# S5 angles on GpSimd, and accumulation groups of u opened by one-pass products with zeros

## The chip, the core and the metric

The kernel runs on one core of one Trainium2 chip, in one launch. The core's engines have queues of their own and wait for each other through semaphores: TensorE (PE in the profile, its weight loads PEld), VectorE (DVE), ScalarE (ACT), GpSimd (POOL) and SyncE (SP), whose queue issues all loads from the chip's memory. The metric is the device time of one execution in microseconds; less is better.

## The reference, cut to what matters

The whole program is a network of three layers over 256 tokens of width 2048 in float32: a state-space layer (S5), a sparse attention layer, and a block with two mixers and a feed-forward part. The change lies in the first, at its beginning:

```
c_act = silu(c)
shift, scale, gate = split(c_act @ mod_w[0] + mod_b[0], 3)
h = rmsnorm(x, norm_g[0]) * (1 + scale) + shift
u, z = split(h @ w_in, 2)
a = exp(lam * dt)            # complex, 128 groups of 64 states; its angle is Im(lam) * dt
x_t = a * x_(t-1) + B u_t    # a scan over the tokens
```

The kernel runs the scan over blocks of four tokens. For it, it needs the angle k * 4 * Im(lam) * dt in turns, brought into -0.5 to 0.5, for k = 0 to 63 and every state: 16 tiles of 128 partitions x 256 columns. These are the S5 angles.

## The kernel before, in words

**The stage of u.** `layer0` makes u, 2048 features x 256 tokens, from h, which is there in 16 pieces h(k) of 128 features. u is held in eight PSUM tiles `ua0` to `ua7` of 128 x 512 while k runs from 0 to 15, and each k adds 16 products (L469, float32, each shown as two records in the trace). So that the two halves of each tile form one accumulation group, a product of a row of zeros with zeros opens it (L448 to L450): `zero` is a tile of one partition and 512 columns, filled by GpSimd, and there is one product of 128 x 512 for each of the eight tiles.

**h(k).** For every k, two vectors of 128 numbers are made from 1 MB of weights each: `mod_ahead` loads a tile `w` of 128 x 2048 (four buffers) and VectorE multiplies it with a row and sums along it (L345, the row product). The first gives the scale (L458 makes A from it), L460 makes `hTf` from x, the second gives the shift, L349 adds the bias, and ScalarE writes h(k) (L463). The weights of u for that k are two loads `wu` of 0.5 MB, three buffers for each half.

**The angles.** Inside the same loop over k stand `s5_angles` for tile k and, for every fourth k, `s5_scaled_b`. In `s5_angles` ScalarE writes two parts of the product, `pa` (kept in `yraw`, four L677 with `fh`) and `pb` (a tile `angb`, four L677 with `fl`), and then five operations of VectorE (L678 to L682) make the sum, its rounded value `pr` (a tile `angr`), the difference, and the limits. `angb` and `angr` have two buffers each. `s5_scaled_b` is six GpSimd operations (L695 to L700), and its two work tiles `bw` are taken from the same buffers as `angb` and `angr`.

**What sets the order.** The program is written as above, and a scheduler orders the instructions of each engine when the kernel is built; after that each engine runs its queue in order. All 64 L677 with `fh` come early; those with `fl` stand between the L463 of the h(k).

**Behind the stage.** u is copied out of PSUM by ScalarE (L488) and VectorE (L486), sent to the chip's memory and read back in another layout; the PSUM tiles are then given to other work, so that the first product of z (L192) comes after the last copy. Three z products stand before the S5 loop over 16 tiles. It reads the angles of tile ut in L783 and L784, which make cosine and sine tables, and for each tile GpSimd, VectorE and ScalarE make small matrices (L743 to L760), the first two tiles' in the stage of u.

Of the kernel before, what the change touches and what calls it, by code (L numbers as in the profile page):

```python
# [10 lines left out]
F32R = mybir.dt.float32r  # L11
I32 = mybir.dt.int32
AF = mybir.ActivationFunctionType
ALU = mybir.AluOpType
# [4 lines left out]
P = 128  # L19
# [4 lines left out]
MAGIC = 12582912.0  # L24
# [15 lines left out]
def build(tc, a, dbg=None, upto=99):  # L40
    with ExitStack() as ctx:
        g = Ctx()
        g.ctx, g.tc, g.nc, g.a, g.dbg = ctx, tc, tc.nc, a, dbg or {}
        setup(g)
        with tc.tile_pool(name="cactp", bufs=1) as g.cactp:
            layer0(g)
            if upto >= 1:
                layer1(g)
        if upto >= 2:
            block2(g, upto)  # L50
        else:
            save_out(g)
            close_x(g)
            if upto:
                g.ucm.__exit__(None, None, None)
            else:
                close_xT(g)
            g.pscm.__exit__(None, None, None)
# [114 lines left out]
def proj_one(g, src, hl):  # L173

    nc = g.nc
    o = g.mm.tile([P, 2, T], F32, name="o", tag="mm")[:, 0, :]
    wk = split_w(g, src, 2048, P)
    for k in range(KD):
        h, l = wk(k)
        nc.tensor.matmul(o, h, hl[:, k, 0, :], start=(k == 0), stop=False)  # L180
        nc.tensor.matmul(o, h, hl[:, k, 1, :], start=False, stop=False)  # L181
        nc.tensor.matmul(o, l, hl[:, k, 0, :], start=False, stop=(k == KD - 1))  # L182
    return o
# [209 lines left out]
def layer0(g):  # L393
    nc, tc, a = g.nc, g.tc, g.a
    V, S, G, E = nc.vector, nc.scalar, nc.gpsimd, nc.tensor
    with ExitStack() as lc:
# [50 lines left out]
        zero = g.sp.tile([P, 512], F32, name="zero", tag="res", bufs=2)[0:1]  # L447
        G.memset(zero, 0.0)  # L448
        for o in acc:
            E.matmul(o, zero[:, 0:P], zero, start=True, stop=False)  # L450
        sc = ExitStack()
        s1 = sc.enter_context(tc.tile_pool(name="l0s1", bufs=1, reuse_waits="tile"))
        with tc.tile_pool(name="l0tmp", bufs=1, reuse_waits="tile") as tmp:
# [1 line left out]
        with tc.tile_pool(name="l0raw", bufs=2, reuse_waits="tile") as rp:  # L455
            for k in range(KD):
                mod_ahead(g, a["mod0"], g.mod0, 16 + k)
                V.scalar_tensor_tensor(out=A0[:, k:k + 1], in0=g.mod0[:, 16 + k:17 + k], scalar=b1[:, k:k + 1], in1=col("norm_g0")[:, k:k + 1], op0=ALU.add, op1=ALU.mult)  # L458
                f = g.sp.tile([P, T], F32, name="hTf", tag="t1k")
                V.scalar_tensor_tensor(out=f, in0=xT[:, k, :], scalar=A0[:, k:k + 1], in1=row, op0=ALU.mult, op1=ALU.mult)  # L460
                mod_ahead(g, a["mod0"], g.mod0, k)
                mod_bias(g, g.mod0, col("mod_b0"), k, k + 1)
                S.activation(out=h[:, k, :], in_=f, func=AF.Identity, bias=g.mod0[:, k:k + 1])  # L463
                for hf, pool in enumerate((g.whp, g.wlp)):
                    w = pool.tile([P, 1024], F32R, name="wu", tag=("wh", "wl")[hf]).bitcast(F32)
                    load = nc.sync.dma_start(out=w, in_=a["w_inu"][k, :, hf * 1024:(hf + 1) * 1024])
                    for i in range(8):
                        m = 8 * hf + i
                        E.matmul(acc[m // 2][:, m % 2, :], w[:, i * P:(i + 1) * P], h[:, k, :], start=False, stop=(k == KD - 1 and m % 2 == 1))  # L469
                s5_angles(g, s5, rp, k, yraw)  # L470
                if k % 4 == 1:
                    s5_scaled_b(g, s5, rp, k // 4, ybuf)
            g.after = load.ins
# [65 lines left out]
        for j in range(KD):  # L539
            o = proj_one(g, a["w_glu"][j], y)  # L540
# [127 lines left out]
def s5_angles(g, R, pool, ut, ang):  # L668

    nc = g.nc  # L670
    tl = lambda nm, sh: pool.tile(sh, F32, name=nm, tag=nm)
    ts4 = slice(4 * ut, 4 * ut + 4)
    pa = ang[:, ut, :].rearrange("p (a k) -> p a k", a=4)
    pb, pr = tl("angb", [P, 4, 64]), tl("angr", [P, 4, 64])
    for i in range(4):
        for f, out in ((R.fh, pa), (R.fl, pb)):
            nc.scalar.activation(out=out[:, i, :], in_=R.km[:, 0, :], func=AF.Copy, scale=f[:, 4 * ut + i:4 * ut + i + 1])  # L677
    nc.vector.tensor_tensor(out=pr, in0=pa, in1=pb, op=ALU.add)  # L678
    nc.vector.tensor_scalar(out=pr, in0=pr, scalar1=MAGIC, scalar2=-MAGIC, op0=ALU.add, op1=ALU.add)
    nc.vector.tensor_tensor(out=pa, in0=pa, in1=pr, op=ALU.subtract)  # L680
    nc.vector.tensor_tensor(out=pa, in0=pa, in1=pb, op=ALU.add)
    nc.vector.tensor_scalar(out=pa, in0=pa, scalar1=0.5, scalar2=-0.5, op0=ALU.min, op1=ALU.max)  # L682


def s5_scaled_b(g, R, pool, q, bb):
# [1128 lines left out]
```

## Time and profile before

| | us |
|---|---|
| median of 3 runs | 2939.35 |
| lowest, highest | 2933.03, 2940.2 |
| the profiled execution | 2936.83 |
| its span, first to last instruction | 2935.0 |
| TensorE busy (matmuls) | 2809.1 |
| VectorE busy | 2064.6 |
| ScalarE busy | 1434.3 |
| GpSimd busy | 478.6 |

The table says which engine has most work over the whole span; which one a stage waits for is another question, and is read from that stage alone. The rows below are therefore almost all of the first 170 us. Times in them are microseconds from the span's start, durations of single operations are in ns where the row says so. A span of GpSimd is rougher than those of the other engines.

### The profile page before, as it was taken

To read this page: it belongs to the slowest core of one execution; us is meant where nothing else is said; L and a number is where in the kernel's file an instruction comes from. 1 tells how busy PE (TensorE), PEld (TensorE's weight loads), DVE (VectorE), ACT (ScalarE), POOL (GpSimd) and SP (SyncE) were. 2 spreads that over 40 slices of the span, in tenths; PEclk is the share of its full clock that TensorE was granted. 3 is DMA by queue.
4 is the path that set the end of the run, shared out by engine and by line. 5 is a ranking of instruction groups with operands and counts; after the bars stand their busy time and mean duration, and the time that the engine had idled before them with its cause. 6 is when DMAs were issued, how large, how long until landed. Compare 5 with 4: busy or idle time off the path is not lost.

```text
span 2935.0 us, 41793 instructions
## 1 busy us (share of the span) xinstructions
PE 2809.1 (96%) x15680; PEld 2425.4 (83%) x15680; DVE 2064.6 (70%) x3400; ACT 1434.3 (49%) x2879; POOL 478.6 (16%) x465
## 2 busy tenths in 40 slices
PE   7989988998999999999999998999999999999998
PEld 5878878876778888888888897788888888888887
DVE  8958897878787777766997685666656665456654
ACT  5337765433345555555555454455444444344443
POOL 1325652210000011012020020111101211002110
PEclk8999988998999999999999999999999999999999
DMA  9964555986975555555544343355655555555553
GB/s 369 394 225 163 182 192 200 351 305 251 338 277 211 199 195 189 204 208 200 184 152 149 125 143 120 127 189 188 231 184 187 187 190 196 187 188 193 193 187 143
DMA packets 111995, 608.75 MB, mean 207 GB/s; under 512 B 27848, under 2 KB 34480, under 8 KB 41648
## 3 DMA queue, kind: packets, MB, share of 16 engines
q1 hardware_dynamic: 111792, 606.08, 57.6%
q8 instruction: 123, 2.02, 0.3%
q14 instruction: 80, 0.66, 0.1%
HBM read 597.23 MB, written 8.79 MB: 206 GB/s over the span
## 4 chain that ended last, share of the span: by engine, by line
PE 76%; DVE 9%; ACT 3%; DMA 3%; issue 2%; POOL 1%; SPq 0%; ACTq 0%; DVEq 0%; POOLq 0%
PE o L168 29%; PE o L169 15%; PE ox L228 6%; PE ox L230 6%; PE ox L229 6%; PE o L1211 2%; DVE wl L143 2%; DVE w L345 2%; PE o L1212 1%; ACT wh L140 1%; PE o L192 1%; DMA w<-in_mod_dram 1%; DMA w<-in_w_kvT_dram 1%; PE o L182 1%; PE o L181 1%
## 5 line engine op out<-in xcount | busy, mean ns | idle before, releaser
L143 DVE TENSOR_TENSOR wl<-w,wh 128x1024 fp32r<-128x1024 f32 x778 | 971.1, 1252 | 645.0 <-ACT wh L140 639.8
L140 ACT CAST wh<-w 128x1024 fp32r<-128x1024 f32 x778 | 812.8, 1048 | 983.1 <-PE o L168 486.0
L168 PE MATMUL o<-u,wh 128*128 128x512 f32 x2704 | 951.0, 395 | 1.0 <-DVE qk L204 0.4
L169 PE MATMUL o<-u,wl 128*128 128x256 f32 x2704 | 761.1, 282 | 2.7 <-DVE ci L1331 2.7
L168 PEld LDWEIGHTS o<-u,wh 128*128 128x128 f32 x2704 | 508.1, 188 | 115.3 <-PE ctr L1343 1.5
L169 PEld LDWEIGHTS o<-u,wl 128*128 128x128 f32 x2704 | 508.4, 188 | 5.1 <-DVE ci L1331 3.1
L168 PE MATMUL o<-hq,wh 128*128 128x512 f32 (+1 forms) x1040 | 374.5, 401 | 3.0 <-DVE hq L339 2.0
L345 DVE SCALAR_TENSOR_TENSOR w<-w,cact 128x2048 f32<-128x2048 f32 x128 | 301.5, 2357 | 41.5 <-DMA w<-in_mod_dram 20.2
L169 PE MATMUL o<-hq,wl 128*128 128x256 f32 (+1 forms) x1040 | 297.5, 286 | 0.0
L168 PEld LDWEIGHTS o<-hq,wh 128*128 128x128 f32 (+1 forms) x1040 | 195.0, 188 | 51.4 <-DVE hq L339 3.4
L169 PEld LDWEIGHTS o<-hq,wl 128*128 128x128 f32 (+1 forms) x1040 | 195.0, 187 | 2.2 <-DVE wl L143 0.2
L228 PE MATMUL ox<-wh,hid 128*128 128x512 f32 x352 | 138.5, 394 | 0.0
L229 PE MATMUL ox<-wh,hid 128*128 128x512 f32 x352 | 137.0, 389 | 0.0
L1190 POOL TENSOR_TENSOR half<-half,gt 128x256 f32<-128x256 f32 x44 | 32.8, 745 | 583.1 <-PE o L168 286.5
L230 PE MATMUL ox<-wl,hid 128*128 128x512 f32 x352 | 125.7, 391 | 0.0
L192 PE MATMUL o<-h,w 128*128 128x256 f32 x512 | 122.9, 395 | 2.1 <-DVE h L486 2.1
L469 PE MATMUL ua<-h,wu 128*128 128x256 f32 x512 | 115.5, 389 | 4.4 <-ACT h L463 4.4
L469 PEld LDWEIGHTS ua<-h,wu 128*128 128x128 f32 x512 | 100.0, 196 | 21.0 <-ACT h L463 5.2
L192 PEld LDWEIGHTS o<-h,w 128*128 128x128 f32 x512 | 99.1, 199 | 15.9 <-DVE h L486 2.5
L168 PE MATMUL o<-hkv,wh 128*128 128x512 f32 x256 | 96.2, 414 | 10.8 <-DVE hkv L339 5.7
L1060 POOL TENSOR_TENSOR om<-om 128x256 f32<-128x256 f32 x16 | 11.8, 734 | 493.9 <-DVE om L1058 341.5
L198 ACT COPY half<-o 128x256 f32<-128x256 f32 (+1 forms) x190 | 68.8, 364 | 30.8 <-PE o L169 27.7
(540 smaller groups left out, 4844.4 us busy)
## 6 DMA issues: line engine op xcount, KB each, us to landing
w<-in_mod_dram SPq DMA_DIRECT2D x96, 1024.0 KB, 6.9
w<-in_w_z_dram SPq DMA_DIRECT2D x48, 1024.0 KB, 4.9
w<-in_w_fg_dram SPq DMA_DIRECT2D x44, 1024.0 KB, 5.0
w<-in_w_fu_dram SPq DMA_DIRECT2D x44, 1024.0 KB, 4.9
w<-in_w_fd_dram SPq DMA_DIRECT2D x44, 1024.0 KB, 4.9
w<-in_kvmod_dram SPq DMA_DIRECT2D x32, 1024.0 KB, 6.3
w<-in_w_out_dram SPq DMA_DIRECT2D x32, 1024.0 KB, 5.6
w<-in_w_qkvz_dram SPq DMA_DIRECT2D x32, 1024.0 KB, 4.9
```

The lines of the kernel that those rows point to most:

```text
L140: nc.scalar.copy(out=wh[:, :step], in_=w)
L143: eng.tensor_tensor(out=wl[:, :step], in0=w, in1=wh[:, :step].bitcast(F32), op=ALU.subtract)
L168: nc.tensor.matmul(o[:m], h, hl[:, k0 + k, :, :], start=(k == 0), stop=False)
L169: nc.tensor.matmul(o[:m, 1, :], l, hl[:, k0 + k, 0, :], start=False, stop=(k == nk - 1))
L192: nc.tensor.matmul(o, w[:, k * P:(k + 1) * P], h[:, k, :], start=(k == 0), stop=(k == KD - 1))
L198: g.nc.scalar.copy(out=t[:m], in_=o[:m, 0, :])
L228: nc.tensor.matmul(ot, h, wh, start=first, stop=False)
L229: nc.tensor.matmul(ot, l, wh, start=False, stop=False)
L230: nc.tensor.matmul(ot, h, wl, start=False, stop=last)
L345: g.nc.vector.scalar_tensor_tensor(out=w, in0=w, scalar=1.0, in1=g.cact, op0=ALU.mult, op1=ALU.mult, accum_out=cols[:, j:j + 1])
L469: E.matmul(acc[m // 2][:, m % 2, :], w[:, i * P:(i + 1) * P], h[:, k, :], start=False, stop=(k == KD - 1 and m % 2 == 1))
L1211: nc.tensor.matmul(o, h[:, sl], hl[k][:, 0, :, :], start=(k == 0), stop=False)
```

## The change

The openers read the zeros as float32r, which TensorE takes in one pass, in place of float32; and the five operations of the angles go from VectorE's queue to GpSimd's:

```
         for o in acc:
-            E.matmul(o, zero[:, 0:P], zero, start=True, stop=False)
+            E.matmul(o, zero[:, 0:P].bitcast(F32R), zero.bitcast(F32R), start=True, stop=False)
...
-    nc.vector.tensor_tensor(out=pr, in0=pa, in1=pb, op=ALU.add)
-    nc.vector.tensor_scalar(out=pr, in0=pr, scalar1=MAGIC, scalar2=-MAGIC, op0=ALU.add, op1=ALU.add)
-    nc.vector.tensor_tensor(out=pa, in0=pa, in1=pr, op=ALU.subtract)
-    nc.vector.tensor_tensor(out=pa, in0=pa, in1=pb, op=ALU.add)
-    nc.vector.tensor_scalar(out=pa, in0=pa, scalar1=0.5, scalar2=-0.5, op0=ALU.min, op1=ALU.max)
+    nc.gpsimd.tensor_tensor(out=pr, in0=pa, in1=pb, op=ALU.add)
+    nc.gpsimd.tensor_scalar(out=pr, in0=pr, scalar1=MAGIC, scalar2=-MAGIC, op0=ALU.add, op1=ALU.add)
+    nc.gpsimd.tensor_tensor(out=pa, in0=pa, in1=pr, op=ALU.subtract)
+    nc.gpsimd.tensor_tensor(out=pa, in0=pa, in1=pb, op=ALU.add)
+    nc.gpsimd.tensor_scalar(out=pa, in0=pa, scalar1=0.5, scalar2=-0.5, op0=ALU.min, op1=ALU.max)
```

The scheduler then orders the other instructions anew too, up to the end of the S5 loop.

GpSimd's queue at the start of the stage, before. The names are those of the kernel with a number for each buffer; `bw_450` and `bw_451` are the work tiles of `s5_scaled_b`.

```order
L448 MEMSET zero_232 1x512
L695 ISA
L695 TENSOR_TENSOR bw_450<-braw_448,cre_339 128x256
L696 TENSOR_TENSOR bw_451<-braw_448,cim_340 128x256
L697 TENSOR_TENSOR ybuf_220<-bw_450,bw_451 128x4x64
L698 TENSOR_TENSOR bw_450<-braw_448,cre_339 128x256
L699 TENSOR_TENSOR bw_451<-braw_448,cim_340 128x256
L700 TENSOR_TENSOR ybuf_220<-bw_450,bw_451 128x4x64
```

The same place now, `angb_387` and `angb_433` being the angles' parts of tiles 0 and 1:

```order
L678 TENSOR_TENSOR angr_388<-yraw_219,angb_387 128x256
L679 TENSOR_SCALAR angr_388<-angr_388 128x256
L678 TENSOR_TENSOR angr_434<-yraw_219,angb_433 128x256
L680 TENSOR_TENSOR yraw_219<-yraw_219,angr_388 128x256
L679 TENSOR_SCALAR angr_434<-angr_434 128x256
L681 TENSOR_TENSOR yraw_219<-yraw_219,angb_387 128x256
L680 TENSOR_TENSOR yraw_219<-yraw_219,angr_434 128x256
L682 TENSOR_SCALAR yraw_219<-yraw_219 128x256
L681 TENSOR_TENSOR yraw_219<-yraw_219,angb_433 128x256
L682 TENSOR_SCALAR yraw_219<-yraw_219 128x256
L695 TENSOR_TENSOR bw_450<-braw_448,cre_339 128x256
L696 TENSOR_TENSOR bw_451<-braw_448,cim_340 128x256
```

The ten operations of the first two tiles stand before `s5_scaled_b`, and the others follow between its groups: 104 operations up to the last angle, where there were 24.

ScalarE's queue towards the end of the stage, before. `hTf_896`, `hTf_942`, `hTf_988` and `hTf_1044` lead to h(11) to h(14); `angb_1071` and `angb_1117` are tiles 14 and 15.

```order
L463 ACTIVATE h_118<-hTf_896,mod0_215 128x256
L677 ACTIVATE angb_1071<-km_350,fl_317 128x64 x4
L463 ACTIVATE h_118<-hTf_942,mod0_215 128x256
L677 ACTIVATE angb_1117<-km_350,fl_317 128x64 x4
L496 COPY d32_1195<-col_116 32x16 x4
L783 ACTIVATE ys_1237<-yraw_219 128x256
L790 ACTIVATE d0_1241<-km_350,r4_296 128x64 x4
L790 ACTIVATE d0_1388<-km_350,r4_296 128x64 x4
L785 ACTIVATE cs_1236<-ys_1237,hpi_325 128x256
L463 ACTIVATE h_118<-hTf_988,mod0_215 128x256
```

The same place now:

```order
L463 ACTIVATE h_118<-hTf_896,mod0_215 128x256
L677 ACTIVATE angb_1015<-km_350,fl_317 128x64 x4
L463 ACTIVATE h_118<-hTf_942,mod0_215 128x256
L677 ACTIVATE angb_1071<-km_350,fl_317 128x64 x4
L677 ACTIVATE angb_1117<-km_350,fl_317 128x64 x4
L463 ACTIVATE h_118<-hTf_988,mod0_215 128x256
L496 COPY d32_1195<-col_116 32x16 x4
L783 ACTIVATE ys_1237<-yraw_219 128x256
L790 ACTIVATE d0_1241<-km_350,r4_296 128x64 x4
L790 ACTIVATE d0_1388<-km_350,r4_296 128x64 x4
L785 ACTIVATE cs_1236<-ys_1237,hpi_325 128x256
L463 ACTIVATE h_118<-hTf_1044,mod0_215 128x256
```

h(13) moved ahead of L496 to L785, h(14) stands behind them; what the L677 before each of them wait for was VectorE (and for some a GpSimd operation of `s5_scaled_b`), and is now GpSimd alone. h(13) stands behind the L677 of tile 15, which needs GpSimd's 95th operation, the last of the fourth `s5_scaled_b`; L496 needs the 100th.

VectorE's queue in the middle of the stage, before: from the second row product of k=8 to the first of k=9.

```order
L345 SCALAR_TENSOR_TENSOR w_750,mod0_215<-w_750,cact_88 128x2048
L678 TENSOR_TENSOR angr_684<-yraw_219,angb_683 128x256
L349 TENSOR_TENSOR mod0_215<-mod0_215,col_116 128x1
L679 TENSOR_SCALAR angr_684<-angr_684 128x256
L680 TENSOR_TENSOR yraw_219<-yraw_219,angr_684 128x256
L681 TENSOR_TENSOR yraw_219<-yraw_219,angb_683 128x256
L682 TENSOR_SCALAR yraw_219<-yraw_219 128x256
L345 SCALAR_TENSOR_TENSOR w_790,mod0_215<-w_790,cact_88 128x2048
```

The same place now, and the next row product:

```order
L345 SCALAR_TENSOR_TENSOR w_750,mod0_215<-w_750,cact_88 128x2048
L349 TENSOR_TENSOR mod0_215<-mod0_215,col_116 128x1
L345 SCALAR_TENSOR_TENSOR w_790,mod0_215<-w_790,cact_88 128x2048
L458 SCALAR_TENSOR_TENSOR A0_216<-mod0_215,b1_217,col_116 128x1
L460 SCALAR_TENSOR_TENSOR hTf_794<-h_118,A0_216,rrow_210 128x256
L345 SCALAR_TENSOR_TENSOR w_796,mod0_215<-w_796,cact_88 128x2048
```

The operations of the angles are gone from between the row products; for each k there are left two L345, L458, L460 and L349.

## Rows read from the trace of the kernel before

**Rows 1.** The page's first line.

```profile
span 2935.0 us, 41793 instructions
```

**Rows 2.** Stretches: length; PE, PEld, DVE, ACT, POOL busy (instructions); PEclk, DMA share, GB/s.

```profile
28.00:42.00 14.00, 13.45 (x17) 5.14 (x16) 12.12 (x43) 10.55 (x36) 0.00 (x0) 0.50 0.88 353
42.00:50.00 8.00, 8.00 (x24) 6.15 (x24) 8.00 (x18) 8.00 (x34) 0.00 (x0) 0.64 0.94 338
50.00:100.00 50.00, 50.00 (x233) 44.03 (x232) 49.21 (x90) 16.89 (x62) 14.86 (x16) 1.00 1.02 404
100.00:150.00 50.00, 49.24 (x227) 42.68 (x226) 49.23 (x79) 16.54 (x58) 23.58 (x21) 1.00 0.99 385
150.00:160.00 10.00, 6.32 (x22) 5.33 (x23) 9.05 (x19) 3.48 (x10) 7.05 (x9) 0.83 0.51 174
```

**Rows 3.** TensorE in order of time: start, us, what, [idle before <-releaser].

```profile
28.64 13.99 PE L450 MATMUL ua<-zero 1*128 1x512 f32 x16 [0.55 <-ACT rrow L327]
...
42.56 92.61 PE L469 MATMUL ua<-h,wu 128*128 128x256 f32 x416
135.68 14.08 PE L469 MATMUL ua<-h,wu 128*128 128x256 f32 x64 [0.52 <-ACT h L463]
153.68 8.79 PE L469 MATMUL ua<-h,wu 128*128 128x256 f32 x32 [3.92 <-ACT h L463]
164.54 20.99 PE L192 MATMUL o<-h,w 128*128 128x256 f32 x96 [2.07 <-DVE h L486]
```

**Rows 4.** VectorE's angle operations and L345: ns min/median/max, first and last start.

```profile
L678 DVE TENSOR_TENSOR angr<-yraw,angb x16: 415/420/834, 55.0 to 129.8; 128x256 f32<-128x256 f32 x16
L679 DVE TENSOR_SCALAR angr<-angr x16: 280/286/707, 55.8 to 130.6; 128x256 f32<-128x256 f32 x16
...
L345 DVE SCALAR_TENSOR_TENSOR w<-w,cact x128: 2227/2285/3341, 15.1 to 1249.1; 128x2048 f32<-128x2048 f32 x128
```

**Rows 5.** Who waited for whom, 50 to 165 us: total, times, longest.

```profile
ACT h L463 <- DVE mod L349: 44.3, 10, 6.4
ACT angb L677 <- DVE yraw L681: 18.1, 9, 4.2
```

**Rows 6.** GpSimd in order of time, `s5_scaled_b`.

```profile
81.38 2.55 POOL L698 TENSOR_TENSOR bw<-braw,cre 128x256 f32<-128x256 f32 x1
...
97.36 0.79 POOL L695 TENSOR_TENSOR bw<-braw,cre 128x256 f32<-128x256 f32 x1 [12.00 <-DVE yraw L682]
...
101.24 2.85 POOL L700 TENSOR_TENSOR ybuf<-bw 128x256 f32<-128x256 f32 x1
```

**Rows 7.** VectorE in order of time, beside GpSimd, and at the stage's end.

```profile
80.64 2.81 DVE L345 SCALAR_TENSOR_TENSOR w<-w,cact 128x2048 f32<-128x2048 f32 x1
...
83.38 0.70 DVE L682 TENSOR_SCALAR yraw<-yraw 128x256 f32<-128x256 f32 x1
84.00 0.57 DVE L458 SCALAR_TENSOR_TENSOR A<-mod,b,col 128x1 f32<-128x1 f32 x1
84.61 1.03 DVE L460 SCALAR_TENSOR_TENSOR hTf<-h,A,rrow 128x256 f32<-128x256 f32 x1
...
161.52 2.28 DVE L345 SCALAR_TENSOR_TENSOR w<-w,cact 128x2048 f32<-128x2048 f32 x1
```

**Rows 8.** GpSimd alone: ns min/median/max of L1060; a memset, busy and mean ns.

```profile
L1060 POOL TENSOR_TENSOR om<-om x16: 724/735/737, 900.9 to 1300.5; 128x256 f32<-128x256 f32 x16
...
L859 POOL MEMSET Vc<- 128x512 f32 x1 | 0.5, 524 | 25.3 <-DVE res L995 25.3
```

**Rows 9.** L345 alone from 53 to 151 us (each shows twice: product and sum).

```profile
53.00:151.00 98.00, 51.55 (x44) 1.00 0.99 395
```

**Rows 10.** ScalarE in order of time.

```profile
51.29 2.00 ACT L677 ACTIVATE angb<-km,fl 128x64 f32<-128x64 f32 x8
...
128.41 0.89 ACT L496 COPY d<-col 32x16 f32<-32x16 f32 x4
...
131.56 0.49 ACT L785 ACTIVATE cs<-ys,hpi 128x256 f32<-128x256 f32 x1
```

## The prediction

> **What bounds the kernel now.** I read the table of stretches first, then TensorE's own order of time, then the waits and the orders of ScalarE, GpSimd and VectorE in the stage that the change touches. The profiled execution spans 2935.0 us [rows 1]; the change lies in its first 170 us, the stage that makes u. TensorE opens the eight accumulation groups from 28.64 to 42.63 us, then runs the u products without a gap: 416 records, 13 values of k, in 92.61 us, so 7.12 us for one k [rows 3]. It waits 0.52 us before k=13 and 3.92 us before k=15, takes 8.79 us for the last k, and is done with u at 162.47 [rows 3]. Both waits end with ScalarE's L463, which writes h(k). The table of stretches says why h comes late: VectorE is busy 49.2 of 50 us in both 50 us stretches [rows 2], and L463 waited 44.3 us in all for VectorE's L349, the bias behind the row product of L345 [rows 5]. The DMA queues are nearly full as well (404 and 385 GB/s [rows 2]). So this stage is bound by VectorE, with the loads and TensorE close behind. A microsecond more or less here moves the end by about as much, since the loop after it cannot start before u is copied out (the first L192 at 164.54 [rows 3]).
>
> **The openers.** Before: 16 records in 13.99 us at a granted clock of 0.50 [rows 2, 3]. No row shows a one-pass opener. The records halve to eight; if a record keeps its 0.87 us (13.99 / 16), the openers take 7.0 us, and TensorE reaches k=0 near 35.6. The bounds are no gain (0) and all of it (14 us). It is worth 7 us only where TensorE stays the last to arrive. From 35.6, k=9 is due at 35.6 + 9 x 7.12 = 99.7 us, or up to 6 us later if the clock stays at 0.50 until 47.8 as now (a mean of 0.64 from 42 to 50 us is 5.8 us at 0.50 [rows 2]). Below, h(9) is not there by then, so I count the openers at nothing. Their cover is the late h; were that gone, they would be worth the 7 us.
>
> **What VectorE gives away.** 16 tiles of five operations: three with two tensors at 0.42 us and two with one tensor at 0.286 us [rows 4], 16 x 1.83 = 29 us of work out of a full engine. If GpSimd ran beside VectorE this would be a clear gain. It doesn't run beside it here.
>
> **What GpSimd takes.** 80 operations are put in front of and between the 24 of s5_scaled_b. Three prices are needed.
> An operation with two tensors: five starts from 97.36 to 101.24 us, with only short VectorE work between, are (101.24 - 97.36) / 5 = 0.776 us apart [rows 6]; alone one lasts 0.735 us [rows 8].
> An operation with one tensor and two constants has no row on GpSimd. Below it lies a plain memset of 128x512 at 0.524 us, half of which is 0.26 us for 256 columns [rows 8]; above it the 0.776 us. VectorE's ratio, 0.286 / 0.42 = 0.68 [rows 4], puts it at 0.53 us, which is what I take, midway between the ends.
> The Trainium skill (GPSIMD Engine Reference, section 3.1, Elementwise — side-by-side cycle accounting) gives a body with one input about 1.03 cycles an element against 2.6 with two. At that page's 1.2 GHz my estimate from it is 0.735 - 256 x 1.57 / 1200 = 0.40 us; the sum below would then be 3.6 us smaller. No run here shows it.
> Third, what a row product costs GpSimd. When L345 (2.285 us [rows 4]) runs, a GpSimd operation that has begun doesn't end until it is over: spans of 2.55 and 2.85 us at 81.38 and 101.24 in place of 0.735 [rows 6], so 1.82 to 2.12 us lost for each L345, 1.95 taken. The reverse also holds: beside GpSimd's operations VectorE's L682, L458 and L460 take 0.70, 0.57 and 1.03 us, one after the other, and the L345 before them 2.81 us [rows 7]. That is about 0.45 us for each GpSimd operation, so 95 of them put 43 us back on VectorE, more than the 29 us taken off. VectorE is not relieved either.
>
> **Where the path goes.** ScalarE's order decides who waits. Its four L677 for tile k write angb, which has two buffers, also used by s5_scaled_b; they wait until GpSimd has read the buffer two uses before. h(k) stands behind them in the same queue. By the order, h(9) stands behind GpSimd's operation 46 of 104, h(13) behind operation 95, and h(14) behind operation 100 and 3.6 us of other ScalarE work (L496 to L785, 128.41 to 132.05 [rows 10]). GpSimd can begin when the first angb is written, about 52.3 us (ScalarE comes to it at 51.29 [rows 10], and nothing before that moves).
> Operation 46: 33 x 0.776 + 13 x 0.53 = 32.5 us, and some 12 row products at 1.95 = 23.4, so 52.3 + 55.9 = 108.2, later than TensorE wants k=9.
> Operation 95: 67 of the two-tensor kind and 28 of the other, 52.0 + 14.8 = 66.8 us. Row products in that time: 22 lie from 53 to 151 us now [rows 9] and are all that remain of the 32; at least 18 must be over, since h(13) itself needs the first 28. I take 20: 39.0 us. 52.3 + 66.8 + 39.0 = 158.1 us. One more group of four L677 (1.0 us) and L463 (0.5 us) give k=13 at about 159.7; it began at 135.68.
> h(14), after five more operations (3.5 us), one or two row products and the 3.6 us, comes at 167 to 169, when k=13 has just ended. Then 3 x 7.12 = 21.4 us, and the 1.7 us that the k after a gap took longer (8.79 against 7.12 [rows 3], the clock 0.83 on the mean in that stretch [rows 2]): u is done at 182.8 in place of 162.47, **20.3 us later**.
> The tail: an L345 that stood at 161.52 before the last two copies of u [rows 7] comes after them, worth at most 0.9 us, left out. GpSimd's work for the first two tiles (L743 to L760) now starts some 20 us later too, near 166, but TensorE needs it only after three z products, 21 us (96 records in 20.99 us [rows 3]) past the end of u: covered by more than 20 us; without that cover it would cost its own 10 us. Behind that, the S5 loop has the same work in a slightly different order; nothing prices that, 0 taken, 8 us either way for the range.
> Against the profiled execution (2936.83 us, of which 2935.0 is the span) the sum is 2957; that execution is 2.5 us under the median of the runs, 2939.35. From the median: 2939.35 + 20.3 = **2960 us**.
>
> **The rivals.**
> A, GpSimd keeps pace: it fits its operations between the row products, ScalarE never waits for it, and VectorE is 20 us ahead. TensorE is then the bound: 35.6 + 16 x 7.12 and 2.9 us for the slow clock at the start (5.8 us at half speed, as above) give 152.4, 10.1 us earlier: 2929 us. For it: VectorE's 99% is what h waits for now. Against it: every L345 that met a waiting GpSimd operation held it to its end. The Trainium skill (SBUF — State Buffer, section Who interferes with whom) says that a VectorE instruction with two inputs in SBUF contends with a GpSimd one that reads SBUF, and that the later one blocks fully; by that rule A is out, and the trace agrees with its 2.85 us.
> B, GpSimd is late, but less: if about half the row products cost it nothing, because it waits for ScalarE or a load at that time anyway, operation 95 comes 10 to 20 us earlier, the openers' 7 us count in part, and u ends within 9 us of now: 2931 to 2948. For it: GpSimd depends on ScalarE's angb, so its idle times may fall under L345.
> C, it is worse: the one-tensor operation costs 1.0 us on GpSimd (28 x 0.47 = 13 us) or the S5 loop loses 8 us by its new order: 2968 to 2981. For it: no row shows that operation on GpSimd.
> Which side it falls on is decided by operation 95: the change is a gain if it is over before about 134 us, a loss after about 142.
>
> **How the numbers follow.** Forecast 0.60, A 0.10, B 0.13, C 0.17. About 0.3%, 9 us, is what a measurement of this kernel can tell from no change. A alone is faster by more than that, B alone within it: faster 0.10, same 0.13, slower 0.77. The forecast's own ends: one-tensor operations at 0.26 or 0.776 us (-7.6, +6.9), 18 or 22 row products (3.9), 1.82 or 2.12 for each (-2.6, +3.4), the S5 loop (8): about 13 us together, 2947 to 2973. The range is widened to take half of B and nearly all of C: 2944 to 2981.
>
> **What would show it.** In the profile after: GpSimd busy nearly throughout from 52 us to beyond 155, with spans of 2.5 us and more on L678 to L682; VectorE's short operations still stretched; ScalarE's L677 waiting for GpSimd's L681 and L700 for tens of us in place of 18.1 us for VectorE [rows 5]; TensorE in gaps before L463 from k=9 on and k=13 near 160; openers of about 7 us. The forecast is wrong if L463 still waits mostly for L349, if angles end before 145, or if TensorE runs u without gaps.

## The result

The changed kernel takes 2960.78 us (median of 6 runs, 2951.64 to 2962.87), and the kernel before in the same comparison 2932.42 us (median of 6, 2925.58 to 2940.2): a ratio of 1.0083, 95% interval 1.0069 to 1.0098. The forecast was 2960 us, slower. It is slower by 28.4 us, where the sum had 20.3 from a median of 2939.35: that the two times lie within 1 us of each other is luck, since the base came out 6.9 us lower than the sum took it and the rise 8.1 us larger. Four of the six runs took 2959 to 2963 us, the traced one among them (2962.74), and two 2952.

The profile after. Its span, then TensorE's order of time (start, duration, line, how many, and in brackets the idle time before and what ended it), against [rows 1, 3]:

```profile
span 2960.9 us, 41771 instructions
```

```profile
29.41 3.75 PE L450 MATMUL ua<-zero 1*128 1x512 f32 x8 [0.55 <-ACT rrow L327]
33.09 44.67 PE L469 MATMUL ua<-h,wu 128*128 128x256 f32 x192
80.56 8.60 PE L469 MATMUL ua<-h,wu 128*128 128x256 f32 x32 [2.81 <-ACT h L463]
92.46 15.77 PE L469 MATMUL ua<-h,wu 128*128 128x256 f32 x64 [3.30 <-ACT h L463]
108.77 7.17 PE L469 MATMUL ua<-h,wu 128*128 128x256 f32 x32 [0.55 <-ACT h L463]
129.97 23.30 PE L469 MATMUL ua<-h,wu 128*128 128x256 f32 x96 [14.02 <-ACT h L463]
160.79 9.44 PE L469 MATMUL ua<-h,wu 128*128 128x256 f32 x32 [7.52 <-ACT h L463]
171.68 14.08 PE L469 MATMUL ua<-h,wu 128*128 128x256 f32 x64 [1.45 <-ACT h L463]
187.94 22.67 PE L192 MATMUL o<-h,w 128*128 128x256 f32 x96 [2.19 <-DVE h L486]
```

The reader sees the openers take 3.75 us in place of 13.99, TensorE begin u 9.5 us earlier, and lose that and more in gaps that all end with L463: 14.02 us before k=10, 7.52 before k=13. u ends at 185.76, and z begins 23.4 us later than before. The waits from 50 to 190 us (us in total, times, longest), against [rows 5], and the table of stretches (the pairs of numbers are TensorE, its weight loads, VectorE, ScalarE and GpSimd, then the granted clock, the DMA share and GB/s), against [rows 2]:

```profile
ACT angb L677 <- POOL yraw L681: 48.3, 7, 9.9
DVE w L345 <- DMA w<-in_mod_dram: 37.7, 14, 10.7
PE ua L469 <- ACT h L463: 29.6, 6, 14.0
ACT angb L677 <- POOL ybuf L700: 20.4, 4, 7.2
```

```profile
50.00:100.00 50.00, 43.90 (x188) 37.51 (x187) 37.74 (x48) 14.06 (x52) 45.58 (x36) 0.93 0.92 364
100.00:150.00 50.00, 35.43 (x153) 30.14 (x152) 23.14 (x27) 8.83 (x32) 48.93 (x52) 0.86 0.71 272
```

L463 no longer waits for L349. ScalarE waits 68.7 us for GpSimd (48.3 + 20.4) with h(k) queued behind it, GpSimd is busy 94.5 of 100 us, and VectorE, which had 98.4 [rows 2], only 60.9. VectorE is idle in large part because its loads are late: it waits 37.7 us for `w`. One reason stands in SyncE's queue (issues, none of them between the second row and the third), and what it does in VectorE's:

```profile
112.52 3.78 SPq L466 DMA_DIRECT2D wu<-in_w_inu_dram  x2
116.40 0.38 SPq L122 DMA_DIRECT2D w<-in_mod_dram  x1
133.66 0.33 SPq L691 DMA_DIRECT2D braw<-in_s5b_dram  x1
134.08 0.38 SPq L122 DMA_DIRECT2D w<-in_mod_dram  x1
...
SPq L691 <- POOL bw L699: 25.2, 3, 16.8
...
139.10 2.30 DVE L345 SCALAR_TENSOR_TENSOR w<-w,cact 128x2048 f32<-128x2048 f32 x1 [10.66 <-DMA w<-in_mod_dram]
```

`braw` has one buffer. Its next load (L691) waits 16.8 us for the late L699 on GpSimd, and the loads of `w` and `wu` behind it in the queue wait with it. It is not the only reason: the same queue waits 58.7 us for TensorE to free buffers of `wu` (L466, shown with the run with four buffers for `braw`). So GpSimd's lateness reaches h by two queues, ScalarE's and SyncE's.

GpSimd itself: the rounding and the clamp (duration in ns, min/median/max), and four of its spans:

```profile
L679 POOL TENSOR_SCALAR angr<-angr x16: 1062/1094/3217, 54.2 to 165.8; 128x256 f32<-128x256 f32 x16
L682 POOL TENSOR_SCALAR yraw<-yraw x16: 393/399/2503, 65.1 to 169.4; 128x256 f32<-128x256 f32 x16
```

```profile
54.24 3.06 POOL L679 TENSOR_SCALAR angr<-angr 128x256 f32<-128x256 f32 x1
57.27 2.67 POOL L678 TENSOR_TENSOR angr<-yraw,angb 128x256 f32<-128x256 f32 x1
59.91 0.72 POOL L680 TENSOR_TENSOR yraw<-yraw,angr 128x256 f32<-128x256 f32 x1
60.60 3.10 POOL L679 TENSOR_SCALAR angr<-angr 128x256 f32<-128x256 f32 x1
```

I added up all of GpSimd's spans on L678 to L700 up to the last angle, and counted as held those over 1.9 us, each with what it has above the shortest of its line: 117.1 us of spans, of which 22 held ones make 42.2 us, 1.92 each. The rest, 74.9 us, is GpSimd's own work.

### The profile page after: what moved, and what is told of

The parts are those of the page before. It is cut to its first block, busy times and chain, and to the rows that moved or that the text cites. A ratio compares the mean times of both kernels' runs of the same rounds, so it can differ in the third digit from the quotient of the medians.

```text
span 2960.9 us, 41771 instructions
## 1 busy us (share of the span) xinstructions
PE 2808.6 (95%) x15672; PEld 2429.6 (82%) x15672; DVE 2042.7 (69%) x3320; ACT 1433.6 (48%) x2879; POOL 564.9 (19%) x545
## 4 chain that ended last, share of the span: by engine, by line
PE 76%; DVE 10%; POOL 5%; ACT 4%; DMA 3%; issue 2%; SPq 0%; ACTq 0%; DVEq 0%; POOLq 0%
PE o L168 29%; PE o L169 15%; PE ox L230 6%; PE ox L228 6%; PE ox L229 6%; PE o L1211 2%; DVE wl L143 2%; DVE w L345 2%; DMA w<-in_mod_dram 1%; PE o L192 1%; PE o L1212 1%; POOL angr L679 1%; PE o L182 1%; PE o L181 1%; PE o L180 1%
## 5 line engine op out<-in xcount | busy, mean ns | idle before, releaser
L345 DVE SCALAR_TENSOR_TENSOR w<-w,cact 128x2048 f32<-128x2048 f32 x128 | 304.9, 2383 | 71.3 <-DMA w<-in_mod_dram 59.3
L469 PE MATMUL ua<-h,wu 128*128 128x256 f32 x512 | 123.0, 405 | 29.6 <-ACT h L463 29.6
L1060 POOL TENSOR_TENSOR om<-om 128x256 f32<-128x256 f32 x16 | 11.8, 735 | 490.4 <-DVE om L1058 341.5
L180 PE MATMUL o<-y,wh 128*128 128x256 f32 x256 | 74.6, 297 | 10.6 <-ACT z L501 4.9
```

The lines of the kernel that those rows point to most:

```text
L345: g.nc.vector.scalar_tensor_tensor(out=w, in0=w, scalar=1.0, in1=g.cact, op0=ALU.mult, op1=ALU.mult, accum_out=cols[:, j:j + 1])
```

## The experiments

The theory going in: the angles alone make the loss; a row product (L345) that meets a GpSimd operation holds it, GpSimd's chain falls behind, and the queues that wait for it bring h late. The rivals: the openers take part in it; GpSimd's own work is simply too much; VectorE, slowed beside GpSimd, is the path. Ratios are against the kernel before on the same chip, with 95% intervals.

**The openers alone.**

```
-            E.matmul(o, zero[:, 0:P], zero, start=True, stop=False)
+            E.matmul(o, zero[:, 0:P].bitcast(F32R), zero.bitcast(F32R), start=True, stop=False)
```

> The kernel before with the one-pass openers alone; the angles stay on VectorE. Theory (the openers were counted at nothing because h is late): TensorE reaches k=0 near 33 us in place of 42.6, runs into a late h from about k=9 on and then follows VectorE, so u ends 0 to 4 us earlier: 2928 to 2933 us against 2932.4. Rival 1 (TensorE is the bound of this stage): the whole 10 us, 2922. Rival 2 (the openers are part of the loss, by the clock of the products behind them): slower than before, 2937 or more.

Measured: 2933.06 us against 2934.02, ratio 0.9993 (0.9981 to 1.0006). TensorE's order of time:

```profile
31.99 64.98 PE L469 MATMUL ua<-h,wu 128*128 128x256 f32 x288
100.28 8.86 PE L469 MATMUL ua<-h,wu 128*128 128x256 f32 x32 [3.31 <-ACT h L463]
110.37 7.17 PE L469 MATMUL ua<-h,wu 128*128 128x256 f32 x32 [1.23 <-ACT h L463]
121.37 29.65 PE L469 MATMUL ua<-h,wu 128*128 128x256 f32 x128 [3.83 <-ACT h L463]
154.31 7.17 PE L469 MATMUL ua<-h,wu 128*128 128x256 f32 x32 [3.29 <-ACT h L463]
162.41 20.99 PE L192 MATMUL o<-h,w 128*128 128x256 f32 x96 [0.92 <-DVE h L486]
```

TensorE starts 10.6 us earlier, runs nine k without a gap, and then gives the lead back in gaps: 3.31 + 1.23 + 3.83 + 3.29 = 11.7 us. z begins 2.1 us earlier than [rows 3] and the time is the same. Counting the openers at nothing was right, and the place (from k=9) too.

**The angles alone.** The five operations go to `nc.gpsimd`, the openers stay in float32.

> The kernel before with the angles on GpSimd alone; the openers stay as they were. Theory (the whole loss comes from the angles, and the openers are hidden behind the late h): as the changed kernel, 2956 to 2963 us, with k=13 near 160 us in the trace. Rival 1 (the openers still gave their 10 us in the changed kernel): 2968 to 2972. Rival 2 (the openers cost something): 2950 or less.

Measured: 2957.32 us, ratio 1.0081 (1.0069 to 1.0093), as with both parts. The loss is that of the angles, and the openers neither help nor hurt beside them. The sign expected in the trace did not come: k=13 begins at 152.34, not near 160; here it is k=14 that is late (166.34, after a gap of 6.83 us), and z begins at 185.08, against 187.94 in the changed kernel.

**The two one-tensor operations back on VectorE.**

```
-    nc.gpsimd.tensor_scalar(out=pr, in0=pr, scalar1=MAGIC, scalar2=-MAGIC, op0=ALU.add, op1=ALU.add)
+    nc.vector.tensor_scalar(out=pr, in0=pr, scalar1=MAGIC, scalar2=-MAGIC, op0=ALU.add, op1=ALU.add)
...
-    nc.gpsimd.tensor_scalar(out=pa, in0=pa, scalar1=0.5, scalar2=-0.5, op0=ALU.min, op1=ALU.max)
+    nc.vector.tensor_scalar(out=pa, in0=pa, scalar1=0.5, scalar2=-0.5, op0=ALU.min, op1=ALU.max)
```

> The changed kernel with the two operations that have one tensor (the rounding L679 and the clamp L682) back on VectorE; the three with two tensors stay on GpSimd. Theory (GpSimd's chain sets the time): it has 16 x (1.06 + 0.40) = 23.4 us less to do, the row products still hold it, and VectorE has 16 x 0.57 = 9 us more: h(13) 8 to 14 us earlier than in the changed kernel, 2946 to 2954 us. Rival (the chain is not the path; VectorE, slowed beside GpSimd, is): VectorE has 9 us more and is slowed by 32 operations fewer, about 14 us, so 2953 to 2961, with L463 waiting for VectorE.

Measured: 2957.47 us, ratio 1.0072 (1.0058 to 1.0085); z begins at 182.01, 5.9 us earlier than in the changed kernel. The theory's number was missed; the rival's number and its sign (L463 waiting for VectorE) came. The waits from 50 to 190 us:

```profile
ACT h L463 <- DVE mod L349: 37.8, 8, 7.3
ACT angb L677 <- POOL yraw L681: 26.1, 5, 7.1
DVE yraw L682 <- POOL yraw L681: 17.5, 11, 3.1
DVE angr L679 <- POOL angr L678: 9.1, 10, 1.5
```

A tile's chain now crosses between the two engines three times. VectorE waits 26.6 us for GpSimd (17.5 + 9.1) in the queue in which the row products and L349 stand; the rival had it slowed by GpSimd, not waiting for its results. GpSimd's part of the angles ends at 146.56 in place of 169.77, and z is only 5.9 us earlier. So the price of L679 on GpSimd can't be read from this run: one wait went and another came.

**Eight buffers for the scratch of the angles.**

```
-        with tc.tile_pool(name="l0raw", bufs=2, reuse_waits="tile") as rp:
+        with tc.tile_pool(name="l0raw", bufs=8, reuse_waits="tile") as rp:
```

> The changed kernel with eight buffers in place of two for the scratch of the angles (and of the rows that share that pool), so that ScalarE's L677 need not wait until GpSimd has read a buffer of two tiles ago, and h(k) does not stand behind that wait. Theory (the buffers are the link between GpSimd and h): L677 stops waiting, h comes as early as VectorE lets it, and u ends within 5 us of the kernel before: 2930 to 2940 us. Rival (VectorE's own operations, held by GpSimd's, delay h as well): L677 stops waiting, but L463 waits for L349 again and h(13) stays near 147 to 152 us: 2945 to 2953.

Measured: 2960.24 us, ratio 1.0080 (1.0068 to 1.0092). Both numbers were missed: the link was cut and next to nothing came of it. In the traced execution (2953.82 us) z begins at 181.78, 6.2 us earlier than in the changed kernel, and L463 waits for L349 again, as the rival had it. The scheduler also used the room to put 16 of the L677 before an h in place of four. The waits (the first three from 50 to 190 us, the last SyncE's from 60 to 165), and one row product:

```profile
ACT h L463 <- DVE mod L349: 51.2, 6, 21.5
DVE w L345 <- DMA w<-in_mod_dram: 33.0, 12, 10.2
ACT angb L677 <- POOL yraw L681: 3.4, 1, 3.4
...
SPq L691 <- POOL bw L699: 43.6, 3, 19.1
...
143.45 9.88 DVE L345 SCALAR_TENSOR_TENSOR w<-w,cact 128x2048 f32<-128x2048 f32 x1 [10.16 <-DMA w<-in_mod_dram]
```

L677's wait for L681 fell from 48.3 to 3.4 us (and for L700 from 20.4 to 10.7), but L691 waits 43.6 us in place of 25.2, so the row products are late, and h behind them. GpSimd, with more ready work, ran without a pause past a row product, which took 9.88 us in place of 2.28.

**Four buffers for `braw`.**

```
-    b = pool.tile([P, 2] + sh[1:], F32, name="braw", bufs=1)
+    b = pool.tile([P, 2] + sh[1:], F32, name="braw", bufs=4)
```

> The changed kernel with four buffers in place of one for braw, so that SyncE's L691 (the load of braw) no longer waits until GpSimd's L699 has read the last one, and the loads of w and wu that stand behind it in SyncE's queue (nothing was issued there from 116.8 to 133.7 us) go out on time. Theory (SyncE's queue, stopped behind a late GpSimd, makes the row products and so h late): VectorE's 37.7 us of waiting for w falls under 15, and u ends 8 to 18 us earlier than in the changed kernel: 2940 to 2953 us. Rival 1 (ScalarE's L677, behind GpSimd's chain, is late enough by itself): the loads come early, L677 still waits some 70 us for GpSimd, 2955 to 2963. Rival 2 (row products that come earlier hold GpSimd's operations more often): later than the changed kernel.

Measured: 2970.76 us, ratio 1.0130 (1.0113 to 1.0147), slower than the changed kernel. SyncE's waits from 50 to 170 us, first of the changed kernel, then of this one:

```profile
SPq L466 <- PE ua L469: 58.7, 20, 7.8
...
SPq L466 <- PE ua L469: 77.2, 19, 10.4
```

The wait of L691 is gone, and that of the loads of `wu` for TensorE grew from 58.7 to 77.2 us; VectorE still waits 32.0 us for `w`. 22 operations of GpSimd are held, as in the changed kernel, so the time of the second rival came, but not for its reason. As I read these waits, the stage is a circle: h late, TensorE late, `wu` buffers free late, SyncE's queue stopped, `w` late, h late; no run takes the circle apart. z begins 1.6 us later than in the changed kernel; the other part of the 10 us lies behind u, where the scheduler's order is another too, and was not followed further.

**Both.**

> The changed kernel with both links cut: four buffers for braw and eight for the scratch of the angles. Neither SyncE nor ScalarE waits for GpSimd in this stage then; what is left is what GpSimd's operations do to VectorE's. Theory (the two queues carry the loss; beside GpSimd a short operation of VectorE loses about 0.33 us, 48 of them 16 us, and a row product about 0.3 us, 32 of them 10 us, which is less than the 29 us taken off VectorE): u ends within 5 us of the kernel before, 2928 to 2938 us. Rival (VectorE loses 0.45 us for each of GpSimd's 104 operations, 47 us, or single row products wait long for a GpSimd that runs without a pause, as the one of 9.88 us in the run with eight buffers alone): 2942 to 2955, L463 waiting for L349.

Measured: 2963.34 us, ratio 1.0105 (1.0089 to 1.0121). Both numbers were missed. VectorE's queue:

```profile
142.53 2.69 DVE L345 SCALAR_TENSOR_TENSOR w<-w,cact 128x2048 f32<-128x2048 f32 x1 [1.18 <-DMA w<-in_mod_dram]
158.47 3.50 DVE L756 TENSOR_TENSOR q<-ybuf,are 128x192 f32<-128x192 f32 x1 [13.24 <-POOL yraw L681]
161.89 0.67 DVE L458 SCALAR_TENSOR_TENSOR A<-mod,b,col 128x1 f32<-128x1 f32 x1
```

A third link: the scheduler put an operation of the first S5 tile (L756), which needs GpSimd, before L458, and VectorE stood 13.24 us. L677 still waits 50.4 us for GpSimd. While GpSimd is late, every queue that holds one instruction depending on it stops the rest; cutting the links one by one is no cure.

**Fewer operations on VectorE, without GpSimd.** A version of my own, which takes the load off VectorE another way.

```
+        nc.scalar.activation(out=pr[:, i, :], in_=R.km[:, 0, :], func=AF.Identity, scale=R.ft[:, c], bias=R.magic)
...
-    nc.vector.tensor_tensor(out=pr, in0=pa, in1=pb, op=ALU.add)
-    nc.vector.tensor_scalar(out=pr, in0=pr, scalar1=MAGIC, scalar2=-MAGIC, op0=ALU.add, op1=ALU.add)
-    nc.vector.tensor_tensor(out=pa, in0=pa, in1=pr, op=ALU.subtract)
-    nc.vector.tensor_tensor(out=pa, in0=pa, in1=pb, op=ALU.add)
+    nc.vector.scalar_tensor_tensor(out=pr, in0=pr, scalar=-MAGIC, in1=pa, op0=ALU.add, op1=ALU.subtract)
+    nc.vector.tensor_tensor(out=pa, in0=pb, in1=pr, op=ALU.subtract)
```

> A version of my own: the one-pass openers, and the angles on VectorE, but with three operations in place of five. ScalarE makes the rounded angle itself (four more activations of 64 columns for a tile: the scale is the unsplit turn, the bias the rounding constant), and VectorE takes off the constant and the first part in one operation, so its add (L678) and its rounding (L679) go: 16 x (0.42 + 0.286) = 11.3 us less on VectorE, 16 x 1.0 us more on ScalarE. Theory (VectorE is the bound of this stage, TensorE next): h comes earlier, TensorE runs u from 32 us with shorter gaps or none, u ends 5 to 10 us earlier than before: 2923 to 2928 us. Rival 1 (the loads are the bound: their share of the DMA engines is 1.02 from 50 to 100 us with the openers alone): 2930 to 2935. Rival 2 (ScalarE's longer queue delays h): slower than before.

Measured: 2936.45 us, ratio 1.0012 (1.0001 to 1.0022): nothing gained. z begins at 161.83, as with the openers alone (162.41). The DMA share is 1.02 and 0.93 in the two 50 us stretches and VectorE is busy 46.5 and 47.4 us, so it was relieved only a little; that the loads then set the pace is my reading of the share, and was not tested. The last gap of TensorE (6.15 us before k=15) is larger than before: VectorE's queue has four operations for the first S5 tiles and a wait of 1.81 us for GpSimd between the last L458 (140.53) and the last row product (146.33), and h(15) is written at 150.28.

**Short row products, in the kernel before and in the changed one.** This takes away what holds GpSimd, and leaves its own work.

```
-    g.nc.vector.scalar_tensor_tensor(out=w, in0=w, scalar=1.0, in1=g.cact, ...)
+    g.nc.vector.scalar_tensor_tensor(out=w[:, 0:n], in0=w[:, 0:n], scalar=1.0, in1=g.cact[:, 0:n], ...)
...
-                mod_ahead(g, a["mod0"], g.mod0, k)
+                mod_ahead(g, a["mod0"], g.mod0, k, 128)
```

> The kernel before, with the row products of the stage of u cut from 2048 to 128 columns (the loads of w stay whole); the rest of each row product is left out. It is the base for the next run. VectorE loses 32 x 2.1 = 67 us of work in this stage; what is left to bind it are the loads (48 MB at some 410 GB/s, 122 us) and TensorE (16 x 7.15 us): u ends 0 to 8 us earlier than in the kernel before, 2924 to 2934 us.

> The changed kernel with the same cut of the row products to 128 columns. Theory (the long row products, which hold a GpSimd operation to their end, are what makes GpSimd late): no span of 2.4 us and more is left on L678 to L682, GpSimd's 104 operations take their own 73 us or so and end by about 130 us, nothing waits long for them, and the time is within 6 us of the kernel before with the same cut. Rival (GpSimd's own work and the queues that wait for it are enough): it stays 15 us or more behind that one.

Measured: 2924.77 us (0.9961, 0.9949 to 0.9973) and 2924.35 us (0.9964, 0.9950 to 0.9978). With the row products short, the change costs nothing. The first row is u in the kernel before with short row products, the others are of the changed one: the stretch from 50 to 100 us, GpSimd's rounding, and z.

```profile
39.12 112.27 PE L469 MATMUL ua<-h,wu 128*128 128x256 f32 x512
...
50.00:100.00 50.00, 50.00 (x233) 44.01 (x232) 14.51 (x42) 15.79 (x57) 48.44 (x70) 1.00 1.02 416
...
L679 POOL TENSOR_SCALAR angr<-angr x16: 1060/1067/1191, 41.9 to 112.9; 128x256 f32<-128x256 f32 x16
...
149.75 20.99 PE L192 MATMUL o<-h,w 128*128 128x256 f32 x96 [0.92 <-DVE h L486]
```

No operation of the angles lasts over 1.2 us, where 3.2 stood; GpSimd gets through 70 instructions in 50 us, where it got through 36; the angles end at 116.05 in place of 169.77. GpSimd is still busy 48.4 of 50 us there, and that does no harm. So its own work fits where no long row products stand beside it. Without the row products in the way, z begins 2.6 us earlier in the changed kernel (149.75 against 152.31), which is all that the two edits are worth there. The cut relieves VectorE as well as GpSimd; that it is GpSimd's release that counts is read from its spans, not from the time alone.

**Every second tile on GpSimd.**

```
+    G = nc.gpsimd if ut % 2 else nc.vector
-    nc.gpsimd.tensor_tensor(out=pr, in0=pa, in1=pb, op=ALU.add)
+    G.tensor_tensor(out=pr, in0=pa, in1=pb, op=ALU.add)
...
```

> The changed kernel with the angles of every second tile on GpSimd and those of the others on VectorE. Theory (a threshold: GpSimd is busy 45.6 and 48.9 of 50 us in the changed kernel, so its queue grows, and the loss comes from that queue): with 40 of the 80 operations it has slack, ends its angles before about 140 us, and at most 8 us of the 28 remain: 2932 to 2942 us. Rival (each operation on GpSimd has its own price): half the loss, 2945 to 2950 us.

Measured: 2946.39 us, ratio 1.0033 (1.0021 to 1.0044): 40% of the loss with half of the operations. That is 10.7 us above the 2935.68 us of the kernel before in this comparison, between the theory's 8 and the rival's 14; the time lies in the rival's range only because that base is 3 us higher than the one the range was made from, and it decides for neither. The angles end at 142.6, and z begins 7.7 us later than before. The rows are one of VectorE's own angle operations (line numbers are one higher here) and z:

```profile
L679 DVE TENSOR_TENSOR angr<-yraw,angb x8: 420/806/941, 52.5 to 126.6; 128x256 f32<-128x256 f32 x8
...
172.22 20.99 PE L192 MATMUL o<-h,w 128*128 128x256 f32 x96 [0.92 <-DVE h L486]
```

Beside a busy GpSimd a VectorE operation of 0.42 us takes 0.81 (the median of eight). GpSimd's spans are 81.3 us, of which 17 held ones make 31.3.

**A quarter of the columns on GpSimd.** The five operations work on `pa[:, 0:1]`, `pb[:, 0:1]` and `pr[:, 0:1]`, one of the four groups of 64 columns; the other three are left without them, and ScalarE fills them with small angles.

> The changed kernel with the five operations of the angles over 64 of the 256 columns on GpSimd; the other 192 columns of an angle are left without them (ScalarE fills them with small angles), so the number of operations and their order on GpSimd stay, and each is shorter. Theory (a threshold, as in the run before): own work of GpSimd falls from 73 to about 40 us, its angles end before 140 us, 2928 to 2940 us. Rival (it is the number of meetings with row products that counts, not the length of the operations): 95 operations still meet some 20 row products, each held for about 2 us, so it ends near 120 to 130 us, ScalarE's L677 still waits some tens of us, and 2940 to 2955.

Measured: 2946.22 us, ratio 1.0034 (1.0018 to 1.0050), in the range of the rival. The waits, the rounding on GpSimd, and TensorE's last gap and z:

```profile
ACT angb L677 <- POOL ybuf L700: 26.0, 4, 8.2
ACT angb L677 <- POOL yraw L681: 14.8, 7, 4.0
...
L679 POOL TENSOR_SCALAR angr<-angr x16: 425/429/2470, 53.7 to 128.1; 128x64 f32<-128x64 f32 x16
...
156.62 9.65 PE L469 MATMUL ua<-h,wu 128*128 128x256 f32 x32 [6.15 <-ACT h L463]
167.19 20.99 PE L192 MATMUL o<-h,w 128*128 128x256 f32 x96 [0.92 <-DVE h L486]
```

The operations are 0.24 to 0.43 us long, GpSimd's own work falls from 74.9 to 44.0 us, but 18 spans are still held, by 36.5 us, against 22 and 42.2 in the changed kernel. What GpSimd loses by being held goes by how many row products find it at work, not by how long its operations are; and L677 still waits 40.8 us.

The trace says more than the median. The traced execution took 2934.95 us (its span is 2933.1, [rows 1] has 2935.0), and z begins in it at 167.19, only 2.7 us later than before, where the changed kernel loses 23.4. GpSimd's 95th operation ends at 123.79 and the angles at 131.62, so that h(13) is written at 132.24 in place of 160.24; the gap of 6.15 us comes after that. So 31 us less of own work, with most of the held time left, take away nearly all of the loss in this stage: own work and held time make GpSimd late together. In the traces the loss of this stage goes without the held time (short row products), and nearly goes without most of the own work. What makes the median of this run 10.5 us longer than that of the kernel before does not lie in what this trace shows, and stays open.

## Why the prediction was right

- **The side and the size.** The forecast's case came, with its mechanism: ScalarE's L677 behind a GpSimd that has more to do and is held by row products. Rival A (GpSimd keeps pace) fell; the rule that spoke against it, of the Trainium skill (SBUF — State Buffer, section Who interferes with whom), agrees with the 3.06 and 3.10 us of operations that take 1.06 alone.
- **The held time.** Predicted 20 x 1.95 = 39.0 us up to operation 95, measured there 20 x 1.90 = 38.0 (22 and 42.2 us up to the last angle). The two runs with short row products show that the loss is gone without this term. It is not the cause by itself: in the traced execution with a quarter of the columns it is nearly all there, and the loss in this stage is 2.7 us.
- **GpSimd's own work.** The sum of the durations held, 68.4 us up to operation 95 for the 66.8 predicted, by two errors that cancel. Two-tensor operations take 0.62 (the first two and the fourth and fifth of `s5_scaled_b`) to 0.72 us, not 0.776. The one-tensor ones were taken at 0.53: the clamp takes 0.40 and the rounding 1.06, above the upper end of 0.776, a mean of 0.73; the price of rival C, 1.0 us, is that of the rounding alone. My estimate from the Trainium skill (GPSIMD Engine Reference, section 3.1, Elementwise — side-by-side cycle accounting) was 0.40 for both: the trace agrees for the clamp and not for the rounding. Operation 95 ended at 159.24, predicted 158.1; k=13 began at 160.79, predicted 159.7.
- **u and z.** u ended at 185.76, predicted 182.8: 1.1 us from k=13's start, and the rest from k=13 itself (9.44 us) and the wait behind it. z begins 23.4 us later, predicted 20.3. Later in the program the same instruction (L959) comes at 892.10 in place of 869.86, 22.2 us; the profiled spans differ by 25.9. The 3 us that come between 1680 and 1880 us, in code that the change doesn't touch, I can't explain; the medians, 28.4 us apart, carry the spread of the runs as well. The S5 loop, taken at 0, cost nothing in this order (and about 8 us in that of the run with four `braw` buffers).
- **The openers.** They take 3.75 us, not 7.0; the price was mis-sized by half, and it didn't matter, since the late h hid them: the run with the openers alone is the same as before. In the changed kernel the first gap comes at k=6, not k=9.
- **VectorE "is not relieved either".** This step failed. It put 0.45 us of delay on VectorE for each of 95 GpSimd operations, 43 us. In the trace after, the L345, L349, L458 and L460 from 50 to 162 us have together 8.8 us above the shortest of their lines, and in the trace before 7.2. The rate came from three rows [rows 7], each of a VectorE operation that was lengthened, and was then charged once for each GpSimd operation. In that stretch of the trace after there are only 57 of these VectorE operations, and 29 of them are as short as the shortest of their line. VectorE was relieved, and then stood idle: 37.7 us of waiting for `w`.
- **SyncE's queue.** The prediction left it out. L691 stands in front of the loads of `w` and `wu`, waits for GpSimd's L699, and stopped that queue for 25.2 us. That it didn't spoil the number is luck: freeing that queue gave nothing in the time, alone or with ScalarE's, and GpSimd's angles end 1.6 and 9.9 us sooner then.
- **The price of a meeting.** The sum treats GpSimd's own work and its held time as two terms that add. The run with a quarter of the columns bears that out: the own work shrank by 31 us and the held time by 6. It also puts the prediction's own test to use, that operation 95 decides the side: over at 159.24, z begins 23.4 us later; over at 123.79, 2.7 us later, which is close to no loss, but not the gain that was said for an end before 134.

No version here beats the kernel before. With the row products short the time falls by 0.4%, and that leaves work out.

## What to carry to other kernels

Before work goes from VectorE to an idle GpSimd, look at what runs on VectorE there: beside long VectorE operations from SBUF, count for each one that meets GpSimd most of its length on GpSimd (here 1.9 of 2.3 us), add GpSimd's own work, and see whether the sum ends before the stage needs it. Then list every queue that holds one instruction waiting for GpSimd, the load queue first. Where several queues wait for the same late engine, freeing one of them only moves the wait to the next; what helped here was less work for GpSimd or nothing long beside it.

## What the runs showed of the hardware

- On GpSimd, with the same shape and type, a one-tensor operation that adds two constants took 1.06 us and one that takes a minimum and a maximum 0.40 us; one with two tensors took 0.72. On VectorE the two one-tensor ones take 0.286 [rows 4] and 0.292. With 64 columns in place of 256 the three took 0.43, 0.24 and 0.32 us, so a column more cost 3.3, 0.8 and 2.1 ns.
- The holding is one-sided in size: a row product of 2.28 us cost a GpSimd operation 1.92 us on the mean, while a short VectorE operation that met GpSimd lost some 0.3 to 0.4 us (0.56 in place of 0.22 for L349, 0.81 in place of 0.42 for an angle operation). One exception: an L345 of 9.88 us, while GpSimd ran without a pause.
- One-pass openers of 128 x 512 took 3.75 us for eight, 0.47 each, at a granted clock of 0.50 (29.4 to 33.1 us), which is 1.2 GHz. With TensorE on the u products from 33 us on, the granted clock was 1.00 (2.4 GHz) from 42 to 50 us, where it was 0.64 on the mean in the kernel before, whose products began at 42.56.
